# Five buffers for each part of the weights, earlier splits, and stores moved to ACT's queue, in a gMLP/SSD/PEER block

## The chip, the cores and the metric

One core of a Trainium2 chip runs the kernel. The metric is the device time of one execution in microseconds (us). An execution of the kernel before takes 3759.26 us in the median of three runs (3750.78 to 3759.49).

The engines are written as in the profile: PE (TensorE, matrix products; PEld are its weight loads), DVE (VectorE), ACT (ScalarE), POOL (GpSimd) and SP (SyncE, which here only starts transfers). Each engine runs its own instructions strictly in the order in which they were laid down, and waits at the first one whose operands or buffers are not ready. A transfer that SP, ACT or POOL starts stands in that engine's order too, and what stands behind it waits as long as it does.

## The reference, cut to what matters

The block works on 1024 tokens of width 1024 (float32).

```
h = x @ w_in                                     # 1024 x (2048 + 2048 + 4096 + 32 + 2048)
uv, z, xbc, dt_raw, gate_pre = split(h)
gates = sigmoid(gate_pre + b_gate)
ya = gmlp_branch(uv, ...) @ gm_w_out             # gelu, layer norm, mixing within chunks of 128 tokens
yb = ssd_branch(z, xbc, dt_raw, ...) @ ssd_w_out # convolution, 32 heads, a state carried over chunks of 128
merged = gates[0] * ya + gates[1] * yb
x1 = layer_norm(ALPHA * x + merged @ w_o)
q = x1 @ peer_w_q                                # 8 heads, two halves, 128 keys each
experts, weights = top 16 of the sums of the two halves' top 16
ch[t] = sum_k weights[t,k] * gelu(u_tab[experts[t,k]] . x1[t]) * v_tab[experts[t,k]]   # 16384 experts
ple = sigmoid(x1 @ ple_w_gate + b) * (p @ ple_w_proj)
out = layer_norm(ALPHA * x1 + ch + ple)
```

## The kernel before

**Tiling.** The tokens go through in three groups (`GROUPS`, L22) of 2, 3 and 3 blocks of 128. For a group, `front` (L215) computes everything up to the choice of experts: the gMLP branch, the SSD branch (16 pairs of heads, `core`, L415), the merge (L513), `w_o` and the first norm (L550 to 574), the queries with their 16 best keys (L587), and the remaining addend (`ple`, L634). For the first two groups the experts' rows are then gathered: POOL fetches 128 rows of 4 KB at a time into a ring of 12 tiles (`gather`, L801; 1280 gathers). Half of them (`peer_u`) are multiplied with x1 on DVE (L822), half (`peer_v`) on PE into `pacc` (L864). This gathering runs beside `front` of the following groups. The third group does not gather: `dense` (L954) multiplies with all 16384 experts' rows in 128 pieces of 128 experts and weights the result with gates that `dense_gates` (L920) has spread out to a full table in DRAM, `g_d`. Of the 128 pieces, 48 are computed ahead (`dense_scores`, L910), stored as `s`, and read back as `ew`.

**Weights.** Every product takes float32 operands in two parts, `hi` and `lo`, and needs three PE passes (`mm3`, L150). `weights` (L138) loads a 512 KB block into `raw` (four buffers), ACT rounds it to `whi` (L146), DVE subtracts to `wlo` (L147); `whi` and `wlo` have three buffers each. A block then serves 24 matmuls (18 in the dense stage's second product `po`). A `raw` load may start when the `wlo` of four blocks earlier is made, and a `whi` may be written when PE has finished the block of three earlier. x itself is split in `prepare` (L199) from tiles of its own, `xraw`.

**Order.** A scheduler lays the instructions of each engine down by a priority, which follows the program's order, and by its own model of when things are ready. `tc.high_priority(offset=n)` lets an instruction stand as if it came n instructions earlier; `AHEAD_W = (20, 20)` (L42) are the offsets of the weights' load and of their split, `AHEAD_G = 40` that of the dense stage's loads. How many gathers go beside which piece of `front` is fixed in the program by `SIDE` and `UNIT` (L1025 to 1036).

**Transfers.** All loads and stores but the gathers are started by SP (`DMA` is `nc.sync`), also the stores of results that ACT or DVE make: `m0` (L348), the SSD states (L452), `yacc` (L486), `x1` (L571), `s` (L917), the gates `g_d` (L952). A state of the group before is loaded in `core` into the tile `pv` (L440) that the pair before it has used.

**The dense stage.** `piece` (L970) takes the gates of four pieces at a time (`GI = 4`): `gte` holds 12 x 4 x 32 values a partition, in two buffers, loaded as runs of 4 x 32 values (512 bytes). The sums `po` go to `eacc` on DVE (L1013).

## Time and profile before

| | |
|---|---|
| median of three runs | 3759.26 us |
| the profiled execution's own time | 3774.55 us |
| its span, first to last instruction | 3772.9 us |
| PE, DVE, ACT, POOL busy | 91%, 78%, 47%, 43% of the span |
| mean granted clock of PE | 0.955 of full speed |
| moved by DMA | 1183.88 MB, 314 GB/s over the span |

Every duration below comes from the one profiled execution. A busy engine is one that executes; PE's matmuls overlap, so a busy PE may still be waiting inside. In a wait list a line reads: engine, the instruction that stood idle before it started, whom it waited for; then us in total, number of times, the longest in us. In a table of stretches a line gives the stretch, its length, and for each engine the busy us and the number of instructions, then PE's granted clock, the share of the 16 DMA engines' time that was in use, and GB/s.

The stages in us from the start: group 0 before its queries 0 to 377; its queries and `ple` and the start of group 1 (with group 0's expert selection) 377 to 660; group 1's gMLP rest and SSD 660 to 1130; its merge, norm, queries and the start of group 2 with group 1's selection 1130 to 1510; group 2's gMLP rest and SSD 1510 to 1980; its norm and queries 1980 to 2360; gates and first scores of the dense form 2360 to 2625; the dense stage with gathers 2625 to 3680, without them 3680 to the end.

### The profile page before, as it was taken

To read this page: it belongs to the slowest core of one execution; us is meant where nothing else is said; L and a number is where in the kernel's file an instruction comes from. 1 tells how busy PE (TensorE), PEld (TensorE's weight loads), DVE (VectorE), ACT (ScalarE), POOL (GpSimd) and SP (SyncE) were. 2 spreads that over 40 slices of the span, in tenths; PEclk is the share of its full clock that TensorE was granted. 3 is DMA by queue.
4 is the path that set the end of the run, shared out by engine and by line. 5 is a ranking of instruction groups with operands and counts; after the bars stand their busy time and mean duration, and the time that the engine had idled before them with its cause. 6 is when DMAs were issued, how large, how long until landed. Compare 5 with 4: busy or idle time off the path is not lost.

```text
span 3772.9 us, 59493 instructions
## 1 busy us (share of the span) xinstructions
PE 3437.7 (91%) x21390; PEld 2946.2 (78%) x21390; DVE 2936.8 (78%) x6823; ACT 1756.0 (47%) x2675; POOL 1606.3 (43%) x1310
## 2 busy tenths in 40 slices
PE   8898997999989988999988989998889989989988
PEld 8897996988877876888878888777667868667756
DVE  6677799898977989896688999997667766766535
ACT  6788543476843333466652334774222323322223
POOL 0000004756545354554354445443556565665540
PEclk9998998999999988999989999999999999999999
DMA  5453656989879886989888899999999999999992
GB/s 200 161 172 130 238 180 241 389 309 356 317 279 385 309 324 234 356 311 343 305 326 327 298 338 349 362 377 372 360 381 400 395 386 389 368 383 401 356 350 95
DMA packets 409159, 1183.88 MB, mean 314 GB/s; under 512 B 41120, under 2 KB 139424, under 8 KB 405792
## 3 DMA queue, kind: packets, MB, share of 16 engines
q0 software_dynamic: 187488, 682.71, 47.7%
q1 hardware_dynamic: 221376, 497.38, 36.9%
q8 instruction: 168, 2.75, 0.3%
q14 instruction: 127, 1.04, 0.1%
HBM read 1121.01 MB, written 58.92 MB: 313 GB/s over the span
## 4 chain that ended last, share of the span: by engine, by line
PE 33%; DVE 16%; DMA 13%; issue 4%; ACT 1%; POOL 1%; SPq 0%; DVEq 0%; ACTq 0%; POOLq 0%
PE mm L152 6%; PE mm L154 6%; PE mm L153 6%; PE pacc L864 4%; DVE row L822 3%; DVE wlo L147 3%; DMA ew<-s 3%; PE po L152 3%; DMA row<-in_peer_v_dram,idxT 3%; PE po L153 3%; PE po L154 3%; DMA raw<-in_peer_uT_dram 2%; PE mt L947 2%; DMA row<-in_peer_u_dram,idx 1%; DMA raw<-in_peer_vd_dram 1%
## 5 line engine op out<-in xcount | busy, mean ns | idle before, releaser
L146 ACT CAST whi<-raw 128x1024 fp32r<-128x1024 f32 (+1 forms) x676 | 701.1, 1041 | 1192.4 <-PE mm L153 612.0
L803 POOL DMA_INDIRECT row<-in_peer_u_dram,idx x640 | 811.5, 1268 | 874.9 <-PE pacc L864 254.3
L147 DVE TENSOR_TENSOR wlo<-raw,whi 128x1024 fp32r<-128x1024 f32 (+1 forms) x676 | 816.2, 1210 | 375.5 <-ACT whi L146 374.7
L154 PE MATMUL mm<-xh,wlo 128*128 128x384 f32 (+2 forms) x3160 | 1056.4, 335 | 46.7 <-DVE wlo L147 46.7
L152 PE MATMUL mm<-xh,whi 128*128 128x384 f32 (+2 forms) x3160 | 1066.3, 338 | 34.3 <-ACT whi L146 25.6
L803 POOL DMA_INDIRECT row<-in_peer_v_dram,idxT x640 | 780.9, 1220 | 712.0 <-PE pacc L864 232.5
L153 PE MATMUL mm<-xl,whi 128*128 128x384 f32 (+2 forms) x3160 | 1051.9, 333 | 0.6 <-DVE xl L136 0.6
L822 DVE SCALAR_TENSOR_TENSOR row<-row,x1b 128x1024 f32<-128x1024 f32 x640 | 774.6, 1217 | 64.8 <-DMA row<-in_peer_u_dram,idx 58.5
L152 PEld LDWEIGHTS mm<-xh,whi 128*128 128x128 f32 (+1 forms) x3160 | 611.2, 194 | 89.7 <-ACT whi L146 46.1
L154 PEld LDWEIGHTS mm<-xh,wlo 128*128 128x128 f32 (+1 forms) x3160 | 609.8, 193 | 66.4 <-DVE wlo L147 55.0
L153 PEld LDWEIGHTS mm<-xl,whi 128*128 128x128 f32 (+1 forms) x3160 | 610.5, 193 | 12.2 <-issue 6.1
L864 PE MATMUL pacc<-row,zw 128*32 128x512 f32 x2560 | 316.9, 614 | 37.0 <-DMA row<-in_peer_v_dram,idxT 36.8
L152 PE MATMUL po<-whi,ewh 128*128 128x512 f32 x768 | 316.0, 411 | 32.2 <-DVE eacc L1013 32.2
L153 PE MATMUL po<-wlo,ewh 128*128 128x512 f32 x768 | 311.0, 405 | 14.4 <-DVE wlo L147 14.3
L154 PE MATMUL po<-whi,ewl 128*128 128x512 f32 x768 | 309.9, 404 | 0.0
L152 PEld LDWEIGHTS po<-whi,ewh 128*128 128x128 f32 x768 | 148.3, 193 | 104.6 <-DVE eacc L1013 36.1
L864 PEld LDWEIGHTS pacc<-row,zw 128*32 128x32 f32 x2560 | 67.9, 111 | 180.6 <-issue 131.1
L135 ACT CAST ewh<-ew 128x384 fp32r<-128x384 f32 x128 | 65.6, 514 | 296.7 <-DVE ew L985 230.1
L818 POOL DMA_DIRECT2D x1b<-x x5 | 3.0, 601 | 446.4 <-DMA x<-x 446.4
L153 PEld LDWEIGHTS po<-wlo,ewh 128*128 128x128 f32 x768 | 148.5, 193 | 51.0 <-DVE wlo L147 16.8
L154 PEld LDWEIGHTS po<-whi,ewl 128*128 128x128 f32 x768 | 148.1, 193 | 40.9 <-issue 5.0
L153 PE MATMUL mm<-wlo,xh 128*128 128x256 f32 x512 | 147.8, 289 | 11.4 <-DVE wlo L147 11.4
(272 smaller groups left out, 5603.8 us busy)
## 6 DMA issues: line engine op xcount, KB each, us to landing
raw<-in_peer_uT_dram SPq DMA_DIRECT2D x128, 512.0 KB, 8.0
raw<-in_peer_vd_dram SPq DMA_DIRECT2D x128, 512.0 KB, 6.8
raw<-in_w_xbc_dram SPq DMA_DIRECT2D x96, 512.0 KB, 5.9
raw<-in_w_g_dram SPq DMA_DIRECT2D x48, 512.0 KB, 6.7
raw<-in_w_z_dram SPq DMA_DIRECT2D x48, 512.0 KB, 5.4
raw<-in_ssd_w_out_dram SPq DMA_DIRECT2D x48, 512.0 KB, 5.3
raw<-in_w_q_dram SPq DMA_DIRECT2D x48, 512.0 KB, 4.7
g<-gt SPq DMA_DIRECT2D x24, 1024.0 KB, 7.5
```

What stands on the lines that cost most here:

```text
L135: A.copy(hi, src)
L146: A.copy(hi, raw)
L147: V.tensor_sub(lo, raw, hi.bitcast(F32))
L152: PE.matmul(p, lhsT=lh, rhs=rh, start=start, stop=False, skip_group_check=skip)
L153: PE.matmul(p, lhsT=lh, rhs=rl, start=False, stop=False, skip_group_check=skip)
L154: PE.matmul(p, lhsT=ll, rhs=rh, start=False, stop=stop, skip_group_check=skip)
L803: g = POOL.indirect_dma_start(out=t, out_offset=None, in_=a[tab], in_offset=bass.IndirectOffsetOnAxis(ap=ix, axis=0))
L818: POOL.dma_start(x1, x1_d[gi, c])
L822: u = V.scalar_tensor_tensor(t, t, 1.0, x1, op0=OP.mult, op1=OP.mult, accum_out=act[:, k:k + 1])
L864: return PE.matmul(pacc[q * 32:q * 32 + 32, h * 512:h * 512 + 512], lhsT=zws[z][:, q, r % 4, :], rhs=ts[q][:, h * 512:h * 512 + 512], star ...
L947: PE.matmul(p[:, i, :], lhsT=o1, rhs=o2, start=True, stop=True)
```

## The change

It does the following.

- `whi` and `wlo` get five buffers each, `raw` three instead of four. The load of a block gets priority offset 150 instead of 20, its split 100 instead of 20.
- `GI` goes from 4 to 2: a `gte` tile holds the gates of two pieces, its load is 384 KB instead of 768 KB, in runs of 256 bytes instead of 512, and there are 64 instead of 32. `ewh`/`ewl` go from 13 to 11 buffers. The additions into `eacc` get priority offset 40.
- Stores of `m0`, the row form of the decay, states, `yacc`, `x1`, `s` and `g_d` go to ACT's queue (118 transfers). The `m0` store of a step is placed after the next step's sigmoid, the state's after the pair's last activation.
- A pair's state of the group before is loaded in `make_x`, with the pair's decay rows, into a tile of its own (`p0`, two buffers).
- In the SSD loop the next group's B and C (`make_bc`) come after the pair's `core` instead of before the next pair's x.
- `prepare` splits x in steps of two through `raw`. Smaller tiles are shared or reused (`ce` is `arow_t`, `sq` is `y`, `yo` is `xin`, `mix` and the softplus' temporaries come from `t1`, `plb` is `lg`, the `ple` result is written over `proj`); the gMLP's spatial weights are loaded by group (`spatial`) instead of at once; `pT` is loaded in the third step of `w_o` into a tile of the gather ring and split after `w_o`; `kT` is loaded two at a time.

```diff
-TC, GI = 32, 4
+TC, GI = 32, 2
...
-AHEAD_W = (20, 20)
+AHEAD_W = (150, 100)
+NRAW, NHI = 3, 5
...
-        raw = wp.tile([128, k, n], F32, name="raw", tag="raw", bufs=4)
-        hi = wp.tile([128, k, n], F32R, name="whi", tag="whi", bufs=3)
-        lo = wp.tile([128, k, n], F32R, name="wlo", tag="wlo", bufs=3)
+        raw = wp.tile([128, k, n], F32, name="raw", tag="raw", bufs=NRAW)
+        hi = wp.tile([128, k, n], F32R, name="whi", tag="whi", bufs=NHI)
+        lo = wp.tile([128, k, n], F32R, name="wlo", tag="wlo", bufs=NHI)
...
-        with tc.tile_pool(name="xr", bufs=4, side=where) as xr:
-            for k in range(KD):
-                raw = xr.tile([128, T], F32, name="xraw")
-                DMA.dma_start(raw, a["xT"][:, k, t0:t0 + T])
-                split(xh[:, k], xl[:, k], raw)
+        for k in range(0, KD, 2):
+            raw = wp.tile([128, 2, T], F32, name="raw", tag="raw", bufs=NRAW)
+            DMA.dma_start(raw, a["xT"][:, k:k + 2, t0:t0 + T])
+            split(xh[:, k:k + 2], xl[:, k:k + 2], raw)
...
+                if late:
+                    A.dma_start(*late.pop())
...
-                DMA.dma_start(m0[j], sg)
+                late.append((m0[j], sg))
...
+                if gi > 0:
+                    pvs[j] = sb.tile([128, 2, 64], F32, name="p0")
+                    DMA.dma_start(pvs[j], state_d[gi - 1, j])
...
-                if gi > 0:
-                    DMA.dma_start(pv[:, 0], state_d[gi - 1, j])
+                p0 = pvs.pop(j, None)
...
-                    DMA.dma_start(state_d[gi, j], pv[:, 0])
...
+                if gi < NG - 1:
+                    A.dma_start(state_d[gi, j], pv[:, 0])
...
-                    DMA.dma_start(yacc[j], o)
+                    A.dma_start(yacc[j], o)
...
-                if j % 2 == 1 and j < 15:
-                    yield from make_bc(j // 2 + 1)
                 if j < 15:
                     yield from make_x(j + 1)
                 if j % 2 == 0:
                     core_g(j // 2)
                 yield from core(j)
+                if j % 2 == 1 and j < 15:
+                    yield from make_bc(j // 2 + 1)
...
+            if u == 2:
+                pT = ring.tile([128, 1024], F32, name="row", tag="row")[:, :2 * T].rearrange(
+                    "p (k t) -> p k t", k=2)
+                DMA.dma_start(pT, a["pT"][:, :, t0:t0 + T])
...
-            DMA.dma_start(s_d[gi, i2], w)
+            A.dma_start(s_d[gi, i2], w)
...
-                    DMA.dma_start(g_d[gi][c, :, b:b + 2048], gf[:, b:b + 2048])
+                    A.dma_start(g_d[gi][c, :, b:b + 2048], gf[:, b:b + 2048])
...
-                ready[i2] = [eb.tile([128, T], F32R, name=n, bufs=I2B + 5) for n in ("ewh", "ewl")]
+                ready[i2] = [eb.tile([128, T], F32R, name=n, bufs=I2B + 3) for n in ("ewh", "ewl")]
...
-                        V.tensor_add(o, o, po[c])
+                        with tc.high_priority(offset=AHEAD_G):
+                            V.tensor_add(o, o, po[c])
```

Three places show what this does to the order. Numbers in names count tiles in program order, so that of one block `raw_n` is followed by `whi_n+1`, and `mm` or `ew` near it by the piece that it serves.

ACT in the middle of the dense stage, before: the scores of one piece (`ew`) and the splits around them.

```order
L146 CAST whi_32306<-raw_32305 128x1024
L146 CAST whi_32348<-raw_32347 128x1024
L983 ACTIVATE ew_32221<-mm_32228 128x384
L135 CAST ewh_32255<-ew_32221 128x384
L146 CAST whi_32378<-raw_32377 128x1024
```

The same place on ACT with the change (the piece is `ew_32214`, its weights are `raw_32215`):

```order
L147 CAST whi_32373<-raw_32372 128x1024
L147 CAST whi_32427<-raw_32426 128x1024
L999 ACTIVATE ew_32214<-mm_32221 128x384
L136 CAST ewh_32248<-ew_32214 128x384
L147 CAST whi_32457<-raw_32456 128x1024
```

When a piece's scores are taken, three later blocks had been split before, five now. Over the whole program ACT's splits lead the block whose sum it reads by 2.2 to 3.0 blocks before and 3.9 to 5.0 with the change, DVE's by 1.6 to 2.1 and 3.2 to 4.0 (means over eighths of the program).

SP at the same place, before: loads of weights in the order of use, and one load of gates, for the pieces from tile number 32538 on.

```order
L144 DMA raw_32222<-in_peer_uT_dram 128x1024
L144 DMA raw_32272<-in_peer_vd_dram 128x1024
L144 DMA raw_32305<-in_peer_uT_dram 128x1024
L144 DMA raw_32347<-in_peer_vd_dram 128x1024
L144 DMA raw_32377<-in_peer_uT_dram 128x1024
L144 DMA raw_32431<-in_peer_vd_dram 128x1024
L975 DMA gte_32538<-g_2_24888 128x12x128
L144 DMA raw_32461<-in_peer_uT_dram 128x1024
```

The same place on SP with the change; the load of gates is for the pieces from tile number 32212 on.

```order
L145 DMA raw_32215<-in_peer_uT_dram 128x1024
L145 DMA raw_32265<-in_peer_vd_dram 128x1024
L145 DMA raw_32298<-in_peer_uT_dram 128x1024
L991 DMA gte_32212<-g_2_24851 128x12x64
L145 DMA raw_32340<-in_peer_vd_dram 128x1024
L145 DMA raw_32372<-in_peer_uT_dram 128x1024
L145 DMA raw_32426<-in_peer_vd_dram 128x1024
L145 DMA raw_32456<-in_peer_uT_dram 128x1024
```

The gates stood ahead of the weights of the piece that they belong to; now they stand three weight loads behind them.

PE at the end of `dense_gates`, before: one-hot products (`mt`, four for a group of four tokens) alternate with the matmuls of score blocks.

```order
L947 MATMUL mt<-o_28101,o_28099 128x128
L153 MATMUL mm<-xl,whi 128x384
L947 MATMUL mt<-o_28106,o_28104 128x128
L154 MATMUL mm<-xh,wlo 128x384
L947 MATMUL mt<-o_28111,o_28109 128x128
L152 MATMUL mm<-xh,whi 128x384
```

The same end on PE with the change:

```order
L963 MATMUL mt<-o_28064,o_28062 128x128
L963 MATMUL mt<-o_28069,o_28067 128x128
L963 MATMUL mt<-o_28074,o_28072 128x128
L880 MATMUL pacc<-row,zw_139 32x512 x8
L153 MATMUL mm<-xh,whi 128x384
```

The last 26 groups of one-hot products (104 matmuls) now stand with nothing between them but a few gathered products; the score matmuls that stood among and behind them have moved ahead. Between the last one-hot product and the first `po` stand 144 score matmuls, where 313 stood.

## Rows read from the trace of the kernel before

**Rows 1.** The page: busy us, share of the span and instructions by engine.
```profile
PE 3437.7 (91%) x21390; PEld 2946.2 (78%) x21390; DVE 2936.8 (78%) x6823; ACT 1756.0 (47%) x2675; POOL 1606.3 (43%) x1310
```
**Rows 2.** Stretches by stage: busy (instructions) of PE, PEld, DVE, ACT, POOL; PEclk, DMA, GB/s.
```profile
0.00:377.00 377.00, 334.63 (x2605) 318.56 (x2606) 254.83 (x546) 290.87 (x479) 0.92 (x7) 0.93 0.49 166
377.00:660.00 283.00, 251.10 (x1827) 239.73 (x1826) 252.55 (x769) 129.24 (x191) 43.88 (x36) 0.95 0.64 220
660.00:1130.00 470.00, 443.20 (x2817) 397.78 (x2816) 407.23 (x763) 285.79 (x438) 265.13 (x188) 0.97 0.89 330
1130.00:1510.00 380.00, 334.34 (x2212) 289.67 (x2211) 331.69 (x1069) 130.39 (x189) 183.57 (x146) 0.93 0.85 313
1510.00:1980.00 470.00, 445.55 (x2905) 385.07 (x2904) 368.33 (x672) 273.96 (x429) 227.21 (x189) 0.97 0.90 328
1980.00:2360.00 380.00, 343.68 (x2172) 312.48 (x2171) 360.24 (x1119) 137.31 (x193) 179.26 (x147) 0.96 0.89 329
2360.00:2625.00 265.00, 240.79 (x1538) 202.74 (x1537) 244.36 (x781) 183.32 (x325) 111.23 (x99) 0.99 0.97 372
2625.00:3680.00 1055.00, 967.10 (x4967) 735.05 (x4969) 667.74 (x1043) 293.83 (x396) 595.07 (x500) 0.95 1.00 378
3680.00:3773.00 93.00, 77.32 (x370) 65.10 (x362) 49.81 (x69) 31.32 (x39) 0.00 (x0) 0.93 0.26 92
```
**Rows 3.** PE's waits over the whole span, the longest in total.
```profile
PE mm L154 <- DVE wlo L147: 46.7, 28, 8.5
PE mm L152 <- ACT whi L146: 39.5, 29, 8.4
PE pacc L864 <- DMA row<-in_peer_v_dram,idxT: 36.8, 13, 8.4
PE po L152 <- DVE eacc L1013: 32.2, 7, 13.5
PE mt L461 <- DVE dec L453: 26.3, 7, 10.7
PE mm L153 <- DVE wlo L147: 23.5, 9, 6.2
PE po L153 <- DVE wlo L147: 14.3, 5, 5.2
```
**Rows 4.** PE's waits between 1980 and 2360 us.
```profile
PE mm L154 <- DVE wlo L147: 13.8, 6, 5.7
PE mm L153 <- DVE wlo L147: 13.7, 5, 6.2
```
**Rows 5.** PE's waits between 0 and 377 us, the first line.
```profile
PE mm L152 <- ACT whi L146: 21.0, 8, 8.4
```
**Rows 6.** Waits of ACT and DVE over the whole span.
```profile
ACT whi L146 <- PE mm L153: 612.0, 239, 10.3
...
DVE wlo L147 <- ACT whi L146: 374.7, 203, 17.7
...
DVE ew L985 <- DMA ew<-s: 82.2, 21, 15.1
...
ACT whi L146 <- DMA raw<-in_peer_uT_dram: 73.8, 12, 17.9
```
**Rows 7.** SP in order of time: start, us, what (one store of scores).
```profile
2603.23 0.32 SPq L917 DMA_DIRECT2D s<-sah  x1
```
**Rows 8.** DMA of 2850 to 2860 us: packets, MB, GB/s, packets by size.
```profile
DMA packets 1129, 4.10 MB, mean 410 GB/s; under 512 B 133, under 2 KB 133, under 8 KB 1127
```
**Rows 9.** The same of 3590 to 3600 us.
```profile
DMA packets 2653, 3.71 MB, mean 371 GB/s; under 512 B 139, under 2 KB 2112, under 8 KB 2651
```
**Rows 10.** DMA issues: transfer, count, KB each, median us to landing.
```profile
gte<-g SPq DMA_DIRECT2D x32, 768.0 KB, 12.2
```
**Rows 11.** Groups of 2180 to 2660 us: one-hot tiles on DVE, busy us, mean ns.
```profile
L945 DVE TENSOR_SCALAR o<-iota,sT 128x128 f32<-128x128 f32 x384 | 129.7, 355 | 0.0
...
L943 DVE TENSOR_SCALAR o<-iota,sT 128x128 f32<-128x128 f32 x288 | 84.2, 293 | 3.7 <-PE mt L947 2.1
```

More of the change, by code (lines that the diff above doesn't have):

```diff
@@ new lines, in front @@
+            raw = wp.tile([128, KD, NCOL], F32, name="raw", tag="raw", bufs=NRAW)
+            DMA.dma_start(raw, a["w_dt"])
+            dh = wp.tile([128, KD, NCOL], F32R, name="whi", tag="whi", bufs=NHI)
+            dl = wp.tile([128, KD, NCOL], F32R, name="wlo", tag="wlo", bufs=NHI)
+            split(dh, dl, raw)
+            pw = psm.tile([NCOL, T], F32, name="mm")
+            for k in range(KD):
+                mm3(pw, (dh[:, k], dl[:, k]), (xh[:, k], xl[:, k]), k == 0, k == KD - 1)
+            dtw = gb.tile([NCOL, T], F32, name="dtw", tag="t1", bufs=3)
@@ L575, in front @@
                 yield 0.5 * unit
+            if mode == "gather":
+                for c in range(NB):
+                    x1_d[gi, c] = dram.tile([128, 1024], F32, name=f"x1_{gi}_{c}")
+                    A.dma_start(x1_d[gi, c], x1[:, c])
             for c in range(NB):
```

188 lines of the change are left out of this document (90 added, 98 removed).

## The prediction

> **What bounds the kernel now.** I began with busy time over the whole span: PE is busy 3437.7 of 3772.9 us [rows 1], so it stands idle for 335 us, and that is the most that any removal of waits can give directly. Then the stages [rows 2], where the reader should compare three columns in each line. From 660 to 1130 and from 1510 to 1980 PE is busy 443 and 446 of 470 us: PE bounds there. From 1980 to 2360 DVE is busy 360 of 380 us and from 2360 to 2625 it is 244 of 265: DVE bounds there, and PE's idle time of 36 and 24 us can shrink only as far as DVE's own idle time, 20 and 21 us. From 2625 to 3680 the DMA engines' share is 1.00: that stage is bounded by transfers. Only the first stage, with DMA at 0.49 and DVE at 255 of 377, has slack everywhere but on PE and ACT.
>
> The wait list of PE says what its idle time is spent on [rows 3]. Waits for a split half of the weights are 46.7 + 39.5 + 23.5 + 14.3 = 124.0 us, 37% of the idle time; 8.4 of them are the kernel's start, when nothing is loaded [rows 5]. Next come gathered rows (36.8), the sums `po` that DVE has not yet taken over (32.2) and the SSD's decay products (26.3). The large lines on ACT and DVE [rows 6] are the same chain seen from its other end: ACT stands 612.0 us because PE still uses the `whi` buffer, DVE 374.7 us because ACT has not rounded. With three buffers the split can never be more than two blocks ahead of PE, and when DVE spends a few us on something else, PE runs dry.
>
> PE's clock is part of the price. The stages show a granted clock of 0.93 to 0.99 [rows 2], lower where PE idles more: 0.93 with 12% idle from 1130 to 1510, 0.97 with 5% from 1510 to 1980. The clock has two levels, 1.2 and 2.4 GHz, so time at the lower one is lost by half. Over the span the lengths times (1 - clock) add up to 173 us in rows 2, some of which is idle time itself: per us of idle between 0 and 173 / 335 = 0.5 us more. I take 0.3.
>
> **The change part by part.** The sum is made against the profiled execution's 3774.55 us, which is 15.3 us above the median; the same difference is then taken from the median.
>
> *Five buffers and earlier splits.* They remove PE's waits for splits outside the dense stage and the start: 124.0 - 14.3 - 8.4 = 101.3 us. The orders show DVE's halves about two blocks further ahead. A block is 24 matmuls, at 443.2 us for 2817 matmuls [rows 2] 0.157 us each, so 3.8 us, and two blocks are 7.6 us of cover; the waits average 1.7 us for the largest line (46.7 over 28) and the longest is 8.5 [rows 3], so nearly all fit. What caps the gain is DVE: from 1980 to 2360 the waits for `wlo` are 27.5 us [rows 4], but DVE has only 20 us of idle time to make splits earlier in, and I give half of the 27.5 there. Elsewhere I give three quarters of the rest: 14 + 0.75 x 73.8 = 69, rounded to 70. Ends: 0 (if the splits stall on something else) and 101. With the clock's share, 0.3 x 70 = 21; ends 0 and 50.
>
> *The dense stage.* Its bound is DMA, so its own waits (14.3 for `wlo`, 32.2 for `po`) are not the measure. A stretch of 4 KB packets alone moves 4.10 MB in 10 us, 410 GB/s [rows 8]. One with 2112 - 139 = 1973 short packets moves 3.71 MB [rows 9]: 0.39 MB less, which at 410 GB/s is 0.95 us of 16 engines, 7.7 ns for each short packet on top of its bytes. The stage moves 378 GB/s x 1055 us = 399 MB, at 410 GB/s 973 us. The gates are 32 loads of 768 KB [rows 10], in runs of 512 bytes 49,152 packets: 49,152 x 7.7 / 16 = 24 us. So today's work needs 997 of 1055 us. Halving the runs doubles the packets. No row shows a 256-byte run. If each costs the same 7.7 ns on top, 24 us are added, a floor of 1021 and at most 34 us to gain. If a 256-byte packet takes as long as one of 512 bytes (20 ns for its bytes at 410 GB/s over 16 engines, and 7.7), 49,152 x 27.7 / 16 = 85 us are added, a floor of 1082 and a loss of 27. Nothing excludes no cost at all, then up to 58. The sum takes the middle of -27 and +34, rounded to +5; the ends are -27 and +58. The Trainium skill (DMA: Bandwidth & Descriptors, "Specifications") speaks against this edit: it asks for transfers of at least 512 bytes for line rate and says that below it the engine does a read-modify-write. By that the upper price holds and the dense term is -27 instead of +5, the sum 53 instead of 85; no run here shows such a packet yet, while its section on small descriptors, with a fixed few cycles a packet, would agree with the 7.7 ns.
>
> *Stores on ACT's queue.* 118 transfers leave SP, where each takes 0.32 us to start [rows 7]: 38 us of instructions on ACT, which is busy 47% [rows 1]. Each stands behind ACT's own result or one made well before, so it adds no long wait; ACT's idle time hides it. What SP no longer waits for lets loads go out earlier, but only the dense stage shows PE or ACT waiting for loads in any number (73.8 us on ACT [rows 6], hidden behind two blocks). I take 0; if the cover were gone, 38 us of ACT would delay splits, which stand four blocks ahead.
>
> *States in their own tile, `make_bc` after `core`.* This touches the decay products' wait, 26.3 us [rows 3], of which single ones of about 10 us stand at the end of a group's loop, where DVE is behind with gathered rows. The state load was one input, DVE's products another. I take +5; ends -10 (B and C now come just in time for the next pair) and +26.
>
> *The start.* x comes in four pieces through three `raw` buffers, and the first weights' load stands behind the fourth piece, which waits for the first split. PE begins at 8.4 us today [rows 5]; I take -3, ends 0 and -5.
>
> *The end of the gates.* The last 26 groups of one-hot products now have no score matmuls beside them. DVE needs for a group at least four second tiles of 0.355 us and three first tiles of 0.293 us [rows 11], 2.3 us; 60 us in which PE has 104 x 0.157 = 16 us of work, and idles for some 40. Against this, 313 - 144 = 169 score matmuls, 27 us, are done before instead of after. As DVE bounds this stage, the work is moved more than lengthened: I take -10, ends -40 and +15.
>
> *x and `pT`.* The loads of x for `w_o` now stand behind `pT`, which waits for a slot of the gather ring, and behind one more load of weights. Two groups, I take -3, ends -12 and 0. The other reused tiles have users that follow each other on one engine anyway: 0.
>
> Sum: 70 + 21 + 5 + 5 - 3 - 10 - 3 = 85 us. The profiled execution would take 3690, the median 3759.3 - 85 = **3674 us**.
>
> **The rivals.**
>
> *The gates come too late* (slower). A `gte` tile now covers two pieces, and its load stands three weight loads behind its piece where it stood ahead. DVE waits in its order for the gates, and behind it stand `wlo`, the `po` additions and the gathered rows. Today the same happens with `ew<-s`: 82.2 us in 21 waits, 3.9 us each [rows 6]. Forty of the pieces read back in the stage would need 20 loads of gates; at 3.9 us each 78 us, and with the upper packet price 27 more, 105 in the dense stage, against 80 gained elsewhere (70 + 21 + 5 - 16): +25, **3784**. It decides once waits for gates in the dense stage pass some 50 us beside the packet price. For it: the DMA share of 1.00 and a landing time of 12.2 us [rows 10]. Against it: half the bytes a load, and a buffer freed several pieces ahead. Chance 0.13. The page's rule above is the other half of this mechanism; without the rule the rival needs 105 us of waits.
>
> *DVE takes the place of PE* (about the same). Where DVE is busy over 87%, earlier splits only push other DVE work later, gathered rows and selections, and POOL's ring empties later. Then only the first stage and the two PE-bound ones give, some 27 us with 8 of clock, less 10 in the dense stage and 15 at the gates' end: -10, **3749**. For it: 360 of 380 us. Against it: the waits are short and bunched, DVE's idle time is elsewhere. Chance 0.15.
>
> *All of it goes* (faster still): 101 + 50 + 34 + 26 + 5 = 216, **3543**. It needs DVE to keep up everywhere and the dense stage at its floor. Chance 0.18.
>
> *The change does not do what it says*: with three `raw` buffers the split stands early in the order but its block is not there, and ACT and DVE wait in their order on the load instead. Today ACT waits 73.8 us for `raw` in 12 waits [rows 6], nearly all where DMA is full. Then some 20 us are gained, **3740**. Chance 0.07.
>
> **How the numbers follow.** The forecast (3600 to 3735) has 0.47. The range should leave out 0.2: above, nearly all of the slower rival (0.13); below, the lower part of the rival that takes all, which reaches 3543. So 3565 to 3765. What a measurement can tell from no change is about 0.3%, 11 us, that is 3748 to 3770. Faster by more: 0.47 + 0.18, half of the DVE rival (0.07) and most of the last (0.05), 0.77. Within: the other half and a rest, 0.10. Slower: 0.13.
>
> **What would show it.** PE's waits for `wlo` and `whi` outside the dense stage should fall from 101 to about 30 us, ACT's wait for PE's buffers should stay in the hundreds. The stretch 1980 to 2360 should shrink by no more than 20 us and DVE there reach 97%. The dense stage should stay within 30 us of 1055, with DMA share at 1.00 and fewer bytes a second where gates are loaded; a stretch with gates alone gives the price of a 256-byte packet. If DVE's wait for gates passes 50 us, the slower rival is at work. If PE waits for splits as before and ACT for `raw`, the last rival is. The prediction is wrong if the time lies in the dense stage, which I have nearly unchanged.

## The result and the profile after

The changed kernel takes 3879.12 us in the median of four runs (3866.13 to 3889.13), the kernel before 3759.38 (3750.78 to 3764.71). The ratio is 1.0319, with a 95% interval of 1.0278 to 1.0359: slower by 3.2%, some 120 us, where 3674 was forecast. The profiled execution took 3866.13 us, with a span of 3864.4; it is the fastest of the four, and that of the kernel before lies 15 us above its median, so the two traces differ by 91 us and not by 120.

The page of the kernel after, busy time by engine and the count of packets:

```profile
PE 3450.5 (89%) x21426; PEld 2960.4 (77%) x21426; DVE 2938.0 (76%) x6832; ACT 1728.2 (45%) x2643; POOL 1567.4 (41%) x1310
DMA packets 461224, 1183.89 MB, mean 306 GB/s; under 512 B 140032, under 2 KB 192256, under 8 KB 457856
```

PE does the same work as before [rows 1], in 13 us more of busy time; most of the loss is idle time, 414 us instead of 335. The packets under 512 bytes have more than tripled, from 41,120 to 140,032.

PE's waits over the whole span (us in total, times, longest us), to be set beside [rows 3]:

```profile
PE po L153 <- DVE eacc L1030: 77.8, 10, 16.1
PE mm L153 <- ACT whi L147: 35.9, 6, 15.9
PE mt L963 <- ACT o L957: 35.1, 21, 6.0
PE pacc L880 <- DMA row<-in_peer_v_dram,idxT: 23.5, 10, 7.5
PE mt L467 <- DVE dec L459: 21.0, 9, 7.5
PE mm L155 <- DVE wlo L148: 17.2, 13, 3.0
```

The waits for splits are down from 124 to 54 us, 28 of these in two places (12.3 at the start, 15.9 at another). What was to go has largely gone. But PE now waits for `eacc` in the dense stage and for ACT's one-hot tiles (`o`) in the gates' stage. The other end of the chain, ACT's waits, to be set beside [rows 6]:

```profile
ACT whi L147 <- PE mm L154: 289.1, 126, 9.8
...
ACT whi L147 <- DMA raw<-in_peer_vd_dram: 191.2, 42, 17.0
ACT whi L147 <- PE po L155: 127.8, 46, 12.2
ACT whi L147 <- DMA raw<-in_peer_uT_dram: 120.9, 39, 11.1
```

ACT used to stand because PE still held the `whi` buffers. Now it stands as much because the block is not loaded: all waits of `whi` for `raw` together are 651 us in 206 waits, 140 in 32 before.

Chips differ: over the chips used here the kernel before takes 3759 to 3798 us in the median. So times are compared as ratios within one set of runs, and stages between kernels on chips where the kernel before takes the same to 0.1%. For this the kernel before and the changed one were profiled once more, on one chip. The table gives, from the start of the first instruction of each kind, the time up to the first one-hot product (everything ahead of the gates), from there to the first `po` (the gates' stage), and from there to the last `po` (the dense stage), in us. All rows are from chips where the kernel before takes 3795 to 3798 us; only the ratio of the changed kernel is from the first chip. Each row of stages is one execution, and executions of one kernel on one chip lie up to 0.6% from their median, so a stage alone is good to some 10 us. Ratios are taken against the kernel before on the same chip, yet they move with the chip too: one run of the changed kernel on the chip of the second set is at 1.026. So differences of about half a per cent or less between sets are not certain.

| kernel | ratio (95%) | to the gates | gates | dense | gates + dense |
|---|---|---|---|---|---|
| before | 1 | 2361.5 | 333.4 | 1095.2 | 1428.6 |
| after | 1.0319 (1.0278 to 1.0359) | 2390.0 | 381.7 | 1106.3 | 1488.0 |
| before, 3 `raw` | 1.0181 (1.0144 to 1.0218) | 2391.9 | 356.2 | 1117.5 | 1473.7 |
| before, GI = 2 | 1.0056 (1.0042 to 1.0070) | 2358.9 | 328.0 | 1108.7 | 1436.7 |
| after, 5 `raw`, 4 split buffers | 1.0048 (1.0030 to 1.0066) | 2341.0 | 375.5 | 1088.8 | 1464.3 |
| after, `s` and gates stored by SP | 1.0297 (1.0264 to 1.0330) | 2388.9 | 347.1 | 1140.6 | 1487.7 |
| after, 5 `raw`, 4 split buffers, GI = 4 | 1.0001 (0.9986 to 1.0016) | 2342.2 | 371.3 | 1070.5 | 1441.8 |
| the same, `s` and gates stored by SP | 0.9970 (0.9955 to 0.9985) | 2344.4 | 336.0 | 1100.0 | 1436.0 |

### The profile page after: what moved, and what is told of

It reads as the page before. It is cut to its first block, busy times and chain, and to the rows that moved or that the text cites. A ratio compares the mean times of both kernels' runs of the same rounds, so it can differ in the third digit from the quotient of the medians.

```text
span 3864.4 us, 59580 instructions
## 1 busy us (share of the span) xinstructions
PE 3450.5 (89%) x21426; PEld 2960.4 (77%) x21426; DVE 2938.0 (76%) x6832; ACT 1728.2 (45%) x2643; POOL 1567.4 (41%) x1310
## 5 line engine op out<-in xcount | busy, mean ns | idle before, releaser
L819 POOL DMA_INDIRECT row<-in_peer_u_dram,idx x640 | 797.5, 1246 | 987.9 <-DVE row L838 314.0
L819 POOL DMA_INDIRECT row<-in_peer_v_dram,idxT x640 | 755.9, 1181 | 744.3 <-DVE row L838 236.5
L963 PE MATMUL mt<-o,o 128*128 128x128 f32 x768 | 151.5, 313 | 47.4 <-ACT o L957 35.1
L1001 DVE TENSOR_TENSOR ew<-ew,gte 128x384 f32<-128x384 f32 x128 | 70.4, 555 | 162.3 <-DMA ew<-s 59.9
L963 PEld LDWEIGHTS mt<-o,o 128*128 128x128 f32 x768 | 124.7, 206 | 80.7 <-ACT o L957 51.0
```

The lines of the kernel that those rows point to most:

```text
L819: g = POOL.indirect_dma_start(out=t, out_offset=None, in_=a[tab], in_offset=bass.IndirectOffsetOnAxis(ap=ix, axis=0))
L963: PE.matmul(p[:, i, :], lhsT=o1, rhs=o2, start=True, stop=True)
L1001: V.tensor_mul(w3, w3, gte[0][:, :, i2 % GI, :])
```

## The experiments

### First set: what makes the loss

Two theories stood at the start. A: the stores on ACT's queue bunch the order of the gates' stage, so that the last 92 one-hot products have no score matmuls beside them. B: splits laid down early make ACT wait for blocks that are not there.

**The old offsets in the changed kernel.**

```
-AHEAD_W = (150, 100)
+AHEAD_W = (20, 20)
```

> The changed kernel with the old offsets (20, 20) for the weights' load and split; five split buffers, stores on ACT's queue and the rest stay. Theory A (the stores of s and of the gates on ACT's queue bunch the order of the gates' stage): the order still leaves 97 one-hot products behind the last score matmul but one, so the stage from the first one-hot product to the first po stays at 350 us or more, and the time at 3850 to 3900. Theory B (splits laid down early make ACT wait for raw blocks that are not there): ACT's waits for raw in the gates' stage fall from 44 to under 10 us, the stage returns to about 310 us, and the time is 3800 to 3830.

Measured: 1.0413 (1.0379 to 1.0446), slower still, against both theories. The time to the gates is 2443.5 us, the gates' stage 398.1, and ACT still waits 47 us there for `raw`. With three `raw` buffers early loads are a help, and B in the form "early is wrong" falls.

**The new offsets in the kernel before.**

```
-AHEAD_W = (20, 20)
+AHEAD_W = (150, 100)
```

> The kernel before with only the offsets (150, 100) for the weights' load and split; four raw buffers, three split buffers, all stores on SP. Theory A: the gates' stage stays at 305 to 320 us; with three split buffers little else can move, 3740 to 3770. Theory B: ACT waits 30 us or more for raw blocks in the gates' stage, the stage takes 340 us or more, and the time is 3790 to 3830.

Measured: 0.9980 (0.9960 to 1.0000); the gates' stage 339.6 us, ACT's waits for `raw` are 71 us in all. With four `raw` buffers the blocks are there, and the offsets are worth at most 15 us. This run has three split buffers; the fourth set comes back to what its waits show.

**Five `raw` and four split buffers in the changed kernel.**

```
-NRAW, NHI = 3, 5
+NRAW, NHI = 5, 4
```

> The changed kernel with five raw buffers and four split buffers instead of three and five (the same memory). Theory A: the gates' stage keeps its bunched order (92 one-hot products behind the last score matmul but one) and stays at 350 us or more, the time at 3860 to 3890. Theory B: the raw blocks are there, ACT's waits for them in the gates' stage fall from 44 to under 15 us, the stage shrinks by 30 us or more, and the time is 3830 or less.

Measured: 1.0048 (1.0030 to 1.0066). Of 3.2% only 0.5 are left: the same memory, given to `raw` instead of `whi` and `wlo`, is worth 2.7% or 103 us (the changed kernel's ratio is from the first chip). ACT's longest waits in this run:

```profile
ACT whi L147 <- PE mm L154: 514.3, 203, 11.8
ACT ewh L136 <- DVE ew L1001: 188.5, 74, 15.2
ACT whi L147 <- issue: 173.8, 61, 12.7
ACT whi L147 <- PE po L155: 147.3, 74, 7.3
```

It waits for PE again and no longer for loads (87 us in 25 waits). But the gates' stage stays at 375.5 us. So B names the main cause, with the number of `raw` buffers and not the earlier placing as its root, and the length of the gates' stage is something else.

**The stores of `s` and of the gates back on SP.**

```
-            A.dma_start(s_d[gi, i2], w)
+            DMA.dma_start(s_d[gi, i2], w)
...
-                    A.dma_start(g_d[gi][c, :, b:b + 2048], gf[:, b:b + 2048])
+                    DMA.dma_start(g_d[gi][c, :, b:b + 2048], gf[:, b:b + 2048])
```

> The changed kernel with the stores of s and of the gates back on SP; the other stores stay on ACT's queue. Theory A: scores and one-hot products alternate again to the end of the gates' stage (1 to 2 one-hot products behind the last scores), the stage returns to about 310 to 325 us, and the time is 3810 to 3835. Theory B: nothing of the early splits changes, the stage stays at 350 us or more, the time within 15 us of 3879.

Measured: 1.0297 (1.0264 to 1.0330), within the interval of the whole change. The stretches of the gates and of the dense stage (length; busy us of PE, PEld, DVE, ACT, POOL; clock, DMA share, GB/s), first of the changed kernel on one chip, then of this run:

```profile
2390.00:2772.00 382.00, 310.73 (x1822) 258.00 (x1821) 300.26 (x882) 204.96 (x362) 164.99 (x144) 0.91 0.91 341
2772.00:3878.00 1106.00, 1002.74 (x5092) 770.82 (x5090) 666.04 (x1031) 303.61 (x408) 549.64 (x460) 0.95 0.94 341
```

```profile
2389.00:2736.00 347.00, 298.07 (x1756) 251.21 (x1755) 282.59 (x852) 207.10 (x362) 125.93 (x114) 0.93 0.88 322
2736.00:3877.00 1141.00, 1016.09 (x5157) 771.68 (x5155) 681.64 (x1061) 303.41 (x408) 583.55 (x491) 0.95 0.95 347
```

The gates' stage loses 35 us and the dense stage gains 34. POOL has 114 instead of 144 instructions in the first and 491 instead of 460 in the second: 30 gathers have changed sides. Theory A's bunching is there, but it moves work over the border between two stages. The lengths of the two taken by themselves mislead; their sum is what counts.

### Second set: single steps of the change in the kernel before

The two whole kernels were profiled on the chip of this set.

> The kernel before, unchanged, on the chip of these runs, so that its stages can be set beside theirs. On the chip of the last runs its median was 3795, 1% over the 3759 of the first chip. If the chip as a whole is slower, all stages are 1% longer (the dense stage 1110 instead of 1099, the time to the first one-hot product 2371 instead of 2348). If a transfer is slower there, only the dense stage is, by some 35 us.

> The changed kernel, unchanged, on the chip of these runs. Its excess over the kernel before should again be 3.2%, some 120 us. Theory R (three raw buffers are too few, and it costs before the gates) puts 60 us or more of it ahead of the first one-hot product; theory P (packets of 256 bytes) puts 40 us or more of it between there and the end. In the first pair of traces it was 33 and 58.

Measured: 3807.73 and 3895.96 us in one run each. The excess is 28.5 us ahead of the gates, 59.4 in the two stages behind: 88 us, not the expected 120. Theory P's 40 behind are there, theory R's 60 ahead of the gates are not. One execution against another can be some 20 us off. The kernel before is not longer by 1% everywhere on this chip: by 13 us ahead of the gates, by 24 in the gates' stage, and its dense stage is 4 us shorter.

**Three `raw` buffers in the kernel before.**

```
-        raw = wp.tile([128, k, n], F32, name="raw", tag="raw", bufs=4)
+        raw = wp.tile([128, k, n], F32, name="raw", tag="raw", bufs=3)
...
-                raw = wp.tile([128, KD, NCOL], F32, name="raw", tag="raw", bufs=4)
+                raw = wp.tile([128, KD, NCOL], F32, name="raw", tag="raw", bufs=3)
```

> The kernel before with three raw buffers instead of four, nothing else. The order is the same as before. Theory R: a raw block is occupied for its load (5 to 8 us from issue to landing), the wait for the split and the split itself (2.3 us), so three of them cannot feed one block each 3.8 us; SP starts loads later, ACT waits for raw blocks (100 us or more over the span, 74 before in all), and the time is longer by 40 to 100 us, a ratio of 1.010 to 1.027. Rival: the split buffers, also three, are what bounds, ACT's waits for PE (612 us) just turn into waits for loads, and the ratio is 0.998 to 1.004.

Measured: 1.0181 (1.0144 to 1.0218), 69 us for one buffer. The first lines of PE's waits, and ACT's for loads:

```profile
PE mm L152 <- ACT whi L146: 69.5, 31, 8.9
PE mm L154 <- DVE wlo L147: 36.8, 29, 8.5
PE mm L153 <- DVE wlo L147: 31.4, 11, 8.9
...
PE po L152 <- ACT whi L146: 24.8, 6, 11.6
```

```profile
ACT whi L146 <- DMA raw<-in_peer_vd_dram: 125.5, 21, 17.5
ACT whi L146 <- DMA raw<-in_peer_uT_dram: 101.0, 23, 16.2
```

PE's waits for `whi` are 94 us where they were 40 on the same chip, ACT's waits for loads 365 us where they were 110. The order was expected to stay the same, and does not quite: the scheduler's model knows the ring's depth, and in the traces 6% of PE's matmuls stand at another place, by 16 places in the mean (a block has 24), and two thirds of ACT's instructions, by three. So the 69 us are the price of the ring with the order that comes with it. All three stages are longer: 30, 23 and 22 us.

Why three are too few can be worked out from rows of the kernel after. A load of 512 KB of the experts' tables lands some 7 us after its issue:

```profile
raw<-in_peer_uT_dram SPq DMA_DIRECT2D x128, 512.0 KB, 7.1
raw<-in_peer_vd_dram SPq DMA_DIRECT2D x128, 512.0 KB, 6.9
```

The cast takes 1.04 us, the subtraction 1.21, so a `raw` buffer is held for 9.3 us when nothing waits for anything, and three of them give, as an estimate, a block each 3.1 us. PE uses one in 3.8 us (24 matmuls at 0.157). A delay of 2 us on ACT or DVE for each block eats that margin; four buffers give one each 2.3 us. ACT's waits for loads show it: 110 us in all with four buffers, 365 with three. SP's waits at a load whose buffer is not free do not. Here they are in the kernel before on this chip (four buffers), in this run (three) and in the changed kernel with five:

```profile
SPq L144 <- DVE wlo L147: 1463.0, 423, 16.9
```

```profile
SPq L144 <- DVE wlo L147: 1448.7, 428, 18.5
```

```profile
SPq L145 <- DVE wlo L148: 1693.4, 423, 24.7
```

SP stands there because loads are laid down before a buffer is free, whether the ring is too small or not.

**GI = 2 in the kernel before.**

```
-TC, GI = 32, 4
+TC, GI = 32, 2
```

> The kernel before with GI = 2 alone: gates loaded for two pieces at a time, in runs of 256 bytes. The order of PE is the same as before. Theory P: the dense stage is bounded by transfers, and 49,152 more packets at 10.7 ns (from the dense stages of the two kernels: 6582 - 6084 us of engine time for 126,785 - 80,432 packets) are 33 us of 16 engines, so 25 to 45 us more, a ratio of 1.007 to 1.012. Rival: the smaller loads are there earlier, DVE's waits for gates and read-back scores shrink by as much as the packets cost, and the ratio is 0.997 to 1.004.

Measured: 1.0056 (1.0042 to 1.0070), 21 us. The packets of the dense stage and SP's queue, kernel before and this run:

```profile
DMA packets 151474, 395.37 MB, mean 361 GB/s; under 512 B 12293, under 2 KB 62981, under 8 KB 151406
...
q1 hardware_dynamic: 80434, 136.07, 34.8%
```

```profile
DMA packets 199477, 396.28 MB, mean 357 GB/s; under 512 B 104800, under 2 KB 110944, under 8 KB 199408
...
q1 hardware_dynamic: 128395, 136.84, 37.3%
```

The queue's packets took 0.348 x 1095 x 16 = 6097 us of engine time, now 0.373 x 1109 x 16 = 6618: 521 us for 47,961 more packets with 0.77 MB more, at most 10.9 ns each, 33 us of 16 engines. The packets' own records in the two traces say a little less: a packet of 256 bytes took 19.0 ns in the mean, one of 512 bytes 29.2, so two for one cost 8.9 ns, 27 us of 16 engines. DVE's waits for `gte` in the dense stage, one of 7.9 us in the whole kernel before, are 24.9 us in 5 waits. Those for read-back scores fall from 84.5 to 67.2. The result lies between the two expectations: the rival (smaller loads make up for it) takes back a part at most.

### Third set: both mended

```
-TC, GI = 32, 2
+TC, GI = 32, 4
...
-NRAW, NHI = 3, 5
+NRAW, NHI = 5, 4
...
-                ready[i2] = [eb.tile([128, T], F32R, name=n, bufs=I2B + 3) for n in ("ewh", "ewl")]
+                ready[i2] = [eb.tile([128, T], F32R, name=n, bufs=I2B + 1) for n in ("ewh", "ewl")]
```

> The changed kernel with five raw and four split buffers (as in the run with 1.0048) and GI = 4 again; ewh and ewl have 9 buffers instead of 11, for the memory. If the two prices found so far (three raw buffers, packets of 256 bytes) are all that the change loses, the ratio to the kernel before is 1.0048 - 0.0056 = 0.999, at most 1.002, and DVE's waits for gates in the dense stage fall from 40 to under 10 us. Rival (the smaller ewh/ewl ring and the earlier additions into eacc are the rest of the loss): 1.004 or more, PE's waits for eacc stay above 60 us.

Measured: 1.0001 (0.9986 to 1.0016). With both steps taken back the loss is gone. PE's waits for `eacc` are still 59.2 us: that part of the rival was right, but it costs no time that shows.

With `NRAW, NHI = 4, 4` and `I2B + 2` instead:

> As the last run, but with four raw and four split buffers, and 10 buffers for ewh and ewl. Theory R in the form that four raw buffers are enough, as in the kernel before: within 0.3% of the run with five, 0.996 to 1.002. Rival (splits laid down early hold a raw block longer, so a fifth is needed): 0.5 to 1.5% over the run with five, and ACT's waits for raw blocks come back (over 150 us).

Measured: 1.0024 (1.0005 to 1.0044), 0.2% over the version with five, with overlapping intervals; ACT's waits for `raw` are 189 us in 54 waits, against 62 in 19. They do come back, but cost little: the fourth `raw` buffer is the one that matters.

With the additions into `eacc` at their place in the program:

```
-                        with tc.high_priority(offset=AHEAD_G):
-                            V.tensor_add(o, o, po[c])
+                        V.tensor_add(o, o, po[c])
```

> As the run with five raw buffers and GI = 4, without the priority offset of the additions into eacc. Theory: PE's waits for eacc (20.7 us before, 73.7 in the run with five raw buffers) come from DVE waiting in its order for gates and read-back scores ahead of the additions; the offset moves the additions forward and helps, without it the waits grow and the ratio is 0.002 to 0.006 higher. Rival: DVE now waits for PE at the additions, the offset costs, and the ratio is 0.003 to 0.008 lower.

Measured: 0.9997 (0.9981 to 1.0013): no difference, and neither theory.

With `s` and the gates stored by SP, as in the first set:

> As the run with five raw buffers and GI = 4, with the stores of s and of the gates back on SP. This restores the alternation of scores and one-hot products. If the bunched order of the gates' stage costs something of its own, the sum of the gates' and the dense stage falls by 10 to 25 us and the ratio is 0.993 to 0.996; if, as in the changed kernel, the work is only moved to the dense stage, gates' stage shorter by some 35 us and dense stage longer by as much, the ratio stays within 0.002.

Measured: 0.9970 (0.9955 to 0.9985), 12 us faster than without. The gates' stage is 35 us shorter, the dense stage 30 longer, the sum 6 less. That lies between the two expectations: most of the work is only moved, a little is gained.

### Fourth set: why the forecast gain does not come even then

In the mended version PE's waits for splits ahead of the gates are largely gone, but the time is the same. PE's longest waits there, of the kernel before and of the mended version (five `raw`, GI = 4):

```profile
PE mm L154 <- DVE wlo L147: 41.2, 21, 6.9
PE mm L152 <- ACT whi L146: 33.1, 24, 8.7
PE mt L461 <- DVE dec L453: 24.8, 7, 9.2
PE mm L153 <- DVE wlo L147: 20.6, 6, 6.2
PE mt L436 <- DVE xdd L433: 11.6, 10, 3.4
```

```profile
PE mm L155 <- DVE wlo L148: 21.1, 13, 5.2
PE mt L467 <- DVE dec L459: 17.2, 10, 6.4
PE mm L802 <- DVE actd L845: 16.5, 2, 15.5
PE mt L444 <- DVE xdd L441: 14.5, 12, 4.2
PE mt L610 <- ACT qT L607: 13.9, 6, 5.7
...
PE mt L763 <- DVE sel L718: 10.4, 2, 6.6
PE mm L153 <- ACT whi L147: 9.8, 1, 9.8
```

Splits: from 96 to 35 us. All waits: from 213 to 201. The rest has grown from 117 to 166 us, on the weights of gathered rows (`actd`), queries, selections, and B and C, which PE now reaches earlier. The time to the gates falls by 19 us.

The same exchange is in the kernel before with the new offsets alone (first set), which has only three split buffers. Its longest waits ahead of the gates:

```profile
PE mt L461 <- DVE dec L453: 43.7, 13, 9.0
PE mm L154 <- DVE wlo L147: 19.5, 12, 5.1
PE mt L581 <- DVE xl L136: 19.4, 5, 8.6
```

Splits are down from 96 to 34 us there, the rest is up from 117 to 174, the ratio 0.9980. So the earlier placing by itself takes most of the waits for splits away, with no more split buffers, and what takes their place does not need the other edits. Is that DVE's load (theory D)?

```
-            u = V.scalar_tensor_tensor(t, t, 1.0, x1, op0=OP.mult, op1=OP.mult, accum_out=act[:, k:k + 1])
+            u = V.scalar_tensor_tensor(t[:, :512], t[:, :512], 1.0, x1[:, :512], op0=OP.mult, op1=OP.mult, accum_out=act[:, k:k + 1])
```

> The kernel before with the product of the gathered peer_u rows formed over 512 of the 1024 columns only: the other half of that sum is left out, so that DVE has less to do (640 instructions of 1.22 us, some 0.5 us less each, 200 us of it before the gates' stage, where DVE is busy 1963 of 2361 us). Theory D (DVE's load decides when weights and decay products are ready): the time to the first one-hot product falls by 30 to 80 us, and PE's waits for split halves there from 96 to 50 us or less. Rival (the small number of split buffers decides): these waits stay above 75 us and the time to the first one-hot product within 20 us of 2361.

> The version with five raw and four split buffers and GI = 4, with the same half of the peer_u sum left out. In the full version PE's waits for split halves before the gates fell from 96 to 35 us, but its waits for DVE's other results grew, and the sum only fell from 213 to 201. Theory D (they grew because DVE, busy at 84%, makes one thing later when it makes another earlier): with less to do they shrink to under 60 us from some 120, the sum falls by 50 us or more, and the time to the first one-hot product by 50 to 100 us from 2342. Rival (these waits are chains of dependent steps and have nothing to do with load): the sum stays within 20 us of 201, and the time to the first one-hot product within 20 us of 2342.

Measured: 0.9836 (0.9812 to 0.9859) for the kernel before with half the sum, 0.9856 (0.9833 to 0.9879) for the mended version. DVE is busy for some 177 us less ahead of the gates. PE's waits for splits there are 74 us in the first, at the rival's edge. In the second all waits are 175 us, 22 of them for splits, so the others are 152 us, against 166 with the full load and 109 in the kernel before with half of it. The growth of 49 us is still 44 when DVE has a tenth less to do, and the mended version gains no more from it (1.45%) than the kernel before (1.64%). The times speak for DVE in part: the first one-hot product comes at 2310.8 us, 37 to 51 earlier than in the two traces of the kernel before, as theory D expected; in the mended version it comes at 2289.2, against 2342.2 on another chip and 2321.2, on the same chip, of the best version below. So DVE's load costs time ahead of the gates, but about as much in both kernels; it does not explain why the other waits grew, as far as a relief of this size tells.

The offsets (20, 20) in the mended version:

> The version with five raw and four split buffers and GI = 4, with the old offsets (20, 20). It tells what the earlier placing of loads and splits is worth when the blocks are there. Theory (five raw buffers are filled ahead in any case; the near split comes too late beside DVE's other work): waits for split halves before the gates rise from 35 to 60 us or more, 15 to 40 us slower, a ratio of 1.004 to 1.010. Rival (DVE bounds, the order of its work changes nothing): 0.998 to 1.002.

Measured: 1.0043 (1.0021 to 1.0066), 16 us slower than with (150, 100). The waits for splits ahead of the gates rise from 35 to 64 us, the others fall from 166 to 146. With full buffers the earlier placing is worth 0.4%: a step of the forecast that holds, at a fifth of its size.

The mended version with both of the last edits of the third set (stores of `s` and gates on SP, additions in place):

> The version with five raw and four split buffers, GI = 4 and the stores of s and of the gates on SP (0.997), without the priority offset of the additions into eacc (0.9997 against 1.0001 with it). If both small gains are real and add up, 0.995 to 0.998; if the second is noise, 0.997.

Measured: 0.9974 (0.9961 to 0.9987), 3753.99 against 3765.22 us. It beats both kernels, by 10 us and by some 130. The second edit adds nothing.

### Fifth set: the change's own order

```
+                if j % 2 == 1 and j < 15:
+                    yield from make_bc(j // 2 + 1)
                 if j < 15:
                     yield from make_x(j + 1)
...
                 yield from core(j)
-                if j % 2 == 1 and j < 15:
-                    yield from make_bc(j // 2 + 1)
```

> The version with five raw and four split buffers, GI = 4, stores of s and of the gates on SP and late eacc additions (0.9974), with B and C of the next group made ahead of the pair's x again, as in the kernel before. Theory O (some of the waits that took the place of the waits for splits come from the change's own order: PE waits 7.3 and 5.4 us for B and C before the gates, none in the kernel before): these two waits vanish, PE's waits for decay products return from 16 to some 25 us, and the time falls by 0 to 10 us, 0.995 to 0.9975. Rival (what PE waits for next is just later by as much): 0.997 to 0.999.

Measured: 1.0029 (1.0010 to 1.0048), 0.55% or 21 us slower than with B and C behind `core`. PE still waits 11.0 us for C, and only 13.4 for decay products. Theory O falls, and the rival missed too: this part of the change seems a gain, although no wait in the list names it. The version with 0.9974 was not run on the chip of this set, so the size of the gain is not certain.

The split's offset 50:

```
-AHEAD_W = (150, 100)
+AHEAD_W = (150, 50)
```

> The version with 0.9974, with the split's offset 50 instead of 100; the loads' offset stays at 150. Theory: the early splits on ACT and DVE push these engines' other results (queries, selections, activations) back; with a split nearer to its use PE's waits for these fall by 10 us or more, those for splits rise by less, and the ratio is 0.993 to 0.996. Rival: the order of DVE differs in few places, and the ratio stays within 0.0015 of 0.9974.

Measured: 1.0012 (0.9997 to 1.0028), 0.4% slower than with 100, with the same doubt about the chip. Waits for splits ahead of the gates rise from 33 to 46 us, those for decay products from 16 to 29. A split nearer to its use does not bring the other results forward here; only with the offsets at (20, 20) were the other waits shorter, 146 us.

## Why the prediction was wrong, step by step

**Its first failure is a term that is missing from the sum.** `raw` went from four buffers to three, and no step priced it. It stood only in the last rival, with a chance of 0.07, as a lesser gain (3740). That rival named the mechanism: ACT waits in its order for loads. Its price, read from ACT's 73.8 us [rows 6], was a price at four buffers. One buffer fewer costs 69 us in the kernel before, and giving two back to `raw` for one pair of split buffers gave 103 us in the changed one. The rival said "the gain is smaller"; what the prediction lacked is the sum of how long a `raw` buffer is held: three of them, for 9.3 us each, give a block each 3.1 us to a PE that uses one in 3.8, and little covers a delay. The test that it set (if ACT waits for `raw` and PE for splits as before) would not have found it either: PE's waits for splits did fall.

**"Five buffers and earlier splits", +70 and +21 for the clock.** The first half of the step held: waits for splits outside the dense stage were to fall from 101 to about 30 us, and in the mended version those ahead of the gates fell to 35. The second half, a wait removed is time gained, failed. The other waits grew by 49 of 61 us, and the time to the gates fell by 19; the offsets are worth 16 us in all. PE's clock ahead of the gates stayed at 0.95, so the 21 us are nothing. Nor were five buffers needed: with three and the new offsets alone the waits for splits are 34 us, so the premise that with three buffers PE runs dry holds only for the old order. The rival "DVE takes PE's place" gave that result (little gained, the waits pass to others); less work on DVE shortens the time to the gates in both kernels alike, so its load does not explain the exchange. What passes the waits on is open. The edits of `pT` (PE waits 7.5 us for `pl`) and of the smaller tiles were not taken apart.

**The dense stage, +5 between -27 and +58.** Measured alone, GI = 2 costs the kernel 21 us, inside the ends; in the one trace the dense stage is 13.5 us longer. Both bounds were worked out from one price a packet: 7.7 ns on top, or 27.7 for a whole packet. It is 9 to 11 ns. The Trainium skill (DMA: Bandwidth & Descriptors, "Specifications") says that the engine does a read-modify-write below 512 bytes; by the upper price that was taken for it 85 us of 16 engines would have gone, and 27 to 33 did. The Trainium skill (DMA: Bandwidth & Descriptors, "Why small descriptors are slow (HBM only)") names a small fixed cost for each packet, which is nearer to what these loads show; by its three cycles beside eight that would be a quarter of the time of a 256-byte packet, and here it is about half (9 of 18 ns). The step chose the middle of its ends for want of a row; the lower price with its full effect, 24 us, since the stage is bounded by transfers, would have been near.

**Stores on ACT's queue, 0.** Taking the stores of `s` and of the gates back gives 12 us in the mended version, and the order is what differs: with them on ACT's queue the scores run ahead of the one-hot products. The prediction saw this in the order and put it under the gates' end. The trace of the kernel after has 165 transfers on ACT's queue, not the 118 that the step counted, 53 us at its own 0.32 us each; what the other stores cost on ACT was not tested.

**The gates' end, -10 between -40 and +15.** The stage grew by 48 us on one chip, but 35 of these went back to the dense stage when the stores were moved. The trace shows 92 one-hot products behind the last scores, not the 104 that the step counted. It is no place where 60 us are lost, though the first pair of traces reads like one.

**States and `make_bc`, +5.** B and C behind `core` alone are worth 21 us, between two chips, inside the ends (-10 and +26).

**The start, -3.** PE began at 12.3 instead of 8.4 us, -4. The step's reason (x goes through three `raw` buffers, and the next weights' load stands behind its last piece) was right and used in one place of three. It also holds where x of the next group is prepared. The three engines in the kernel after, at the `ple` weights of the second group (start us, us; idle before):

```profile
1327.59 0.38 SPq L211 DMA_DIRECT2D raw<-in_xT_dram  x1
1328.45 15.94 SPq L145 DMA_DIRECT2D raw<-in_ple_w_gate_dram  x6
```

```profile
1325.74 2.30 ACT L136 CAST xh<-raw 128x768 fp32r<-128x768 f32 x3 [13.51 <-DMA vi<-vi]
1335.75 0.83 ACT L136 CAST xh<-raw 128x768 fp32r<-128x768 f32 x1 [7.72 <-DMA raw<-in_xT_dram]
1337.61 1.04 ACT L147 CAST whi<-raw 128x1024 fp32r<-128x1024 f32 x1 [1.02 <-DMA raw<-in_ple_w_gate_dram]
```

```profile
1338.70 0.58 PE L153 MATMUL mm<-whi,xh 128*128 128x256 f32 x1 [15.89 <-ACT whi L147]
```

Three pieces of x hold all three buffers until ACT casts them at 1325.74. Only then go the fourth piece (1327.59) and the weights' load (1328.45) out, and PE stands for 15.89 us. With five `raw` buffers this wait is gone from the list.

**The slower rival (gates come too late)** is in the traces: DVE's waits for `gte` went from 5.2 to 58.3 us. It had been priced with the packets at 105 us; GI = 2 costs 21 in all, and taking it back gives 18 (1.0048 to 1.0001).

Forecast and measured, in us gained:

| step | forecast | measured |
|---|---|---|
| `raw` 4 to 3 | not in the sum | -69 alone, -103 in the changed kernel (with 5 to 4 split buffers) |
| earlier splits and more buffers, with the clock | +91 | 16 by the offsets; 19 to the gates in all |
| dense stage (GI = 2) | +5 | -21 for the whole kernel |
| ACT's queue and the gates' end | -10 | -12 |
| `make_bc` | +5 (with the states) | +21, between two chips |

The rows were measured in different company and don't add up to a sum. The order of their sizes is what they show.

## What to carry to other kernels

A ring of buffers is sized by how long one is held (load, wait and use together) against how often one is needed. The engine behind the ring, waiting for loads, tells that it is too small (110 us with four buffers, 365 with three); the queue that waits for a free buffer does not (1463 and 1449 us). Of the two rings of this chain the memory was worth more in front, at the slow transfer. A wait of the busiest engine that goes away is time gained only as far as its next inputs are ready too: add up all its waits in a version where it is gone, not the ones that were aimed at. Where a change moves work over the border between stages, read the sum of both.

## What the runs showed of the hardware

Loading the same bytes in packets of 256 instead of 512 bytes costs 9 to 11 ns of an engine's time for each packet more (8.9 by the packets' own records, 10.9 by the queue's share of time), near the 7.7 ns by which short packets stood out in the kernel before [rows 8, 9]. In the trace of the run with GI = 2 alone the packets of SP's queue take, in the median, 18 ns for 256 bytes, 27 for 512, 46 for 1024, 84 for 2048 and 159 for 4096: by an estimate from these, some 9 ns for the packet and 37 ns for each KB. No jump stands between 512 and 256 bytes. One program differs by 1% between chips (3759 to 3798 us in the median), and not evenly: the kernel before needed 24 us more in its gates' stage and 4 less in its dense stage on the second chip.
